# Token groups of 64, 64, 69 and 69 chunks, and the SSM's products of one round in alternating PSUM banks

## The chip, the core and the metric

The kernel runs on one core of a Trainium2 chip. The metric is the device time of one execution in microseconds (us), lower is better; "the time" of a kernel is the median of its runs. TensorE is called PE here (its weight loads PEld), VectorE DVE, ScalarE ACT, GpSimd POOL; SP is the engine whose queue issues all the DMAs.

## The reference

One step of a hybrid decoder layer over 2064 prompt tokens (16 meta tokens and 2048 others) and 8 running sequences of 8 tokens, 1024 features, all in float32.

```python
xn = rmsnorm(h, norm_gain)
u_s, z_s, u_p, z_p, gates = split(xn @ w_in)            # six blocks of 1024 columns
y_s = S5(u_s)        # 64 groups of 16 channels, 64 complex states each, then gelu and a GLU (w_glu)
y_p = pool(u_p)      # causal means over 2, 4, 8, 16 tokens, then pool_mix and pool_scale
merged = g_s * ((y_s * silu(z_s)) @ w_branch_ssm) + g_p * ((y_p * silu(z_p)) @ w_branch_pool)
out = rmsnorm(h + merged @ w_out, final_norm_gain)      # and the new SSM states and pool rows
```

## The kernel before

**Tokens.** Eight consecutive tokens make a chunk. The 258 chunks of the prompt and the 8 running sequences (one chunk each) are 266 columns, cut into four groups `g0` to `g3` of 69, 69, 64 and 64 chunks (`GROUPS`), so of 552, 552, 512 and 512 token columns. The first two chunks of `g0` are the meta tokens; only the SSM's input `us` and the pool's input `up` are computed for them, so the other products of `g0` have 67 chunks, 536 columns. A group of more than 512 columns does each matmul in two halves (`nh = 2`: 2 x 276, or 2 x 268 in `g0`), one of at most 512 in one piece (`nh = 1`). The last group holds the running sequences, and does its last three output units in two halves (`HD`), so that the end of one half can overlap the other.

**Units.** The work of a group is a row of units: 80 products with a 128 x 1024 block of weights (`us`, `up`, `zp`, `gate`, `brp`, `zs`, `glu`, `brs`, `out`, eight of each, and eight more gates), and four smaller `mix` units. A product is done in three parts to keep float32's precision (`mm3`: high weights by high and by low data, low weights by high data). So a unit is 8 x 3 matmuls, or 8 x 3 pairs of halves; a `mix` unit is 12. That makes 80 x 24 + 4 x 12 = 1968 such steps for each group. ACT makes each weight block's high part (`wh`, L106), DVE its low part (`wl`, L207), two units ahead. PE's results lie in three accumulators (`acc`); what reads one is called its post (`po`, `H`, `E`, ...), and a unit can't start before the post of the third unit back is done.

**Order.** Everything is written out in one order by hand: the `us` units of `g1` and of `g0`, then the rest of `g0`, of `g1`, `g2`, `g3`. The `us` units of `g2` and `g3` lie within `g0`. Other work is put between the matmuls of a unit (`between`):
- The matrices stage (`batches`, lines 349 to 458): beside `g0`'s pool units (`up`, `zp`, `mix`), 16 batches build the SSM's per-group matrices. For each, DVE, POOL and PE do a fixed set of operations (`bt`, `ct`, `t`, `t4b`, `ps_bt`, `ps_k`) that does not depend on the groups' sizes.
- The SSM (lines 463 to 625): 32 pairs of channel groups, in two rounds (`ROUNDS`). Round 0 covers the chunks of `g0` and `g1` (138 columns) and runs within `g0`, round 1 covers `g2` and `g3` (128) and runs within the last units of `g0`, in `g1` and in the first part of `g2`. A pair goes through steps of a pipeline, one tick each: load; the product x (`st_x`, PSUM tile `sx`); turn (`st_turn_a`, `st_turn_v`: ACT and DVE read `sx`); scan; swap; rot; state (POOL writes `sS`); the product y (`st_y`, tile `sy`); out (`st_out`: ACT reads `sy`, SP stores it). In each tick the steps in `EARLY` come first (the readers `st_out` and `st_turn_*`), those in `LATE` after them (`st_y`, then `st_x`). `sx` and `sy` have one PSUM bank each, so the x of a pair waits until DVE has read the x of the pair before, and y until ACT has.

SP's queue issues its DMAs in the order of the program, and each waits for its buffer. In round 1 the running sequences' old states `s0` were loaded with the pair's input, behind it in the tile `su`, and POOL copied them into `sS`.

Of the kernel before, what the change touches and what calls it, by code (L numbers as in the profile page):

```python
# [34 lines left out]
RK = (2.0 * DM) ** (2.0 / 3.0)  # L35


GROUPS = [(0, 69), (69, 69), (138, 64), (202, 64)]
GOFF = [T * k0 for k0, _ in GROUPS]

ROUNDS = [(0, 138), (138, 128)]


W_US, W_ZS, W_UP, W_ZP, W_GS, W_GP, W_GLU, W_BRS, W_BRP, W_OUT = range(0, 80, 8)
# [45 lines left out]
def hybrid_step(ctx, tc, a):  # L90
# [393 lines left out]
        return rows.rearrange("(q c) t k -> (c t) q k", q=2)  # L484

    def st_load(g, q):
        x = stile("su", 5, g.kn + (NS if g.last else 0))
        u = x[:, :, :g.kn]
        for i in (2 * g.i, 2 * g.i + 1):
            k = GROUPS[i][0] - ROUNDS[g.i][0]  # L490
            SY.dma_start(u[:, :, k:k + GROUPS[i][1]], chans(us_d[i], q))
        if g.last:
            SY.dma_start(x[:, :, g.kn:], a["s0"][:, 0, two(q)])
        mb = stile("smb", 2, P)
        SY.dma_start(mb, mat_d[q, :, 0])
        pr[q].update(u=u, mb=mb, s0=x[:, :, g.kn:])

    def st_phase(g, q):
        ph, n = stile("sph", 4), stile("scc", 4)
# [17 lines left out]
    def st_x(g, q):  # L517

        d = pr[q]
        d["px"] = sw["sx"][:, :, :g.kn]  # L520
        for j in range(2):
            PE.matmul(d["px"][:, j], d["mb"][:, j], d["u"][:, j], start=True, stop=True)  # L522

# [51 lines left out]
    def st_state(g, q):  # L575

        d = pr[q]
        c, w, kp = d["c"], d["s"], g.kp
        s = stile("sS", 3, g.kn)
        now = state[:, two(q)].unsqueeze(2)  # L580
        if g.last:
            G.tensor_copy(s[:, :, kp:], d["s0"])
        G.tensor_copy(s[:, :, 0:1], now)
        G.tensor_tensor(s[:, :, 1:kp], c[:, :, 1:kp], w[:, :, 1:kp], ALU.subtract)
        G.tensor_tensor(now, c[:, :, kp:kp + 1], w[:, :, kp:kp + 1], ALU.subtract)
        d["S"] = s

    def st_y(g, q):
        d = pr[q]
        d["py"] = sw["sy"][:, :, :g.kn]  # L590
        for j in range(2):
            m = slice(j * P, (j + 1) * P)
            PE.matmul(d["py"][:, j], d["m"][:, 0, m], d["u"][:, j], start=True, stop=False)  # L593
            PE.matmul(d["py"][:, j], d["m"][:, 1, m], d["S"][:, j], start=False, stop=True)  # L594
# [40 lines left out]
    class Group:  # L635
# [42 lines left out]
        def proj(self, w, xh, xl, halves=None, meta=False):  # L678


            ps = self.acc()
            n = self.HD if halves else self.ND
            nk = len(xh)
            for k in range(nk):
                between(k / nk)
                outs, xs = [], []
                for h in halves or range(self.nh):
                    m = n + (T * self.km if meta and h else 0)
                    outs.append(ps[:, h, :m])
                    xs.append([v[k][:, h * n:h * n + m] for v in (xh, xl)])  # L690
                mm3(outs, [x[:, k * P:(k + 1) * P] for x in w], xs, k == 0, k == nk - 1)
            return ps
# [63 lines left out]
        def rms_sum(self, ss, halves=None, early=False):  # L756

            n = self.HD if halves else ss.shape[1] // self.nh
            if early:
                ps = [psb.tile([P, 512], F32, tag=t, name=t)[:, :n] for t in ("bx", "by")]  # L760
            else:
                acc = self.acc()
                ps = [acc[:, h, :n] for h in range(self.nh)]
            for h in halves or range(self.nh):
                PE.matmul(ps[h], onesm, ss[:, h * n:(h + 1) * n], start=True, stop=True)  # L765
            self.ps = ps
# [54 lines left out]
        def up_post(self, fb, ps):  # L821
            wi = fb // 2
            kn, kp, last = self.kn, self.kp, self.last
            ke = 2 + kp + (3 * NS if last else 0)
            own = sw["r"] if last else tmp
            E = self.t(own, "E", 2, shape=[P, T, ke])
            if last:
                es = E[:, :, 2 + kp:].rearrange("p t (s k) -> p t s k", k=3)
                G.tensor_copy(es[:, :, :, 0:2], self.hs.pop(fb))
            if last:  # L830
                src = ps[:, 0, :self.N].rearrange("p (t k) -> p t k", k=kn)
                A.activation(E[:, :, 2:2 + kp], src[:, :, :kp], AF.Copy)
                A.activation(es[:, :, :, 2:3], src[:, :, kp:].unsqueeze(3), AF.Copy)
            else:
                for dst, src in self.parts(E[:, :, 2:2 + kp], ps):
                    A.activation(dst, src, AF.Copy)  # L836
            G.tensor_copy(E[:, :, 0:2], hist[:, fb])
            if last:
                new = self.t(own, "np", 2, shape=[P, T, 2 + NS])
                G.tensor_copy(new[:, :, 0:2], E[:, :, kp:kp + 2])  # L840
                G.tensor_copy(new[:, :, 2:].unsqueeze(3), es[:, :, :, 2:3])
                SY.dma_start(a["np"][:, fb], new)
            else:
                G.tensor_copy(hist[:, fb], E[:, :, kp:kp + 2])  # L844
            cur = E
            for step in range(wi + 1):
                d = 1 << step
                nxt = self.t(own, f"w{step % 2}", 1, shape=[P, T, ke])

                if d < 4:  # L850
                    n, o, c = (x.rearrange("p t k -> p (t k)") for x in (nxt, cur, cur))
                    i = d * ke + step
                    V.tensor_tensor(n[:, i:], o[:, i:], c[:, step:T * ke - d * ke], ALU.add)  # L853
                elif d < T:
                    V.tensor_tensor(nxt[:, d:, 1:], cur[:, d:, 1:], cur[:, :T - d, 1:], ALU.add)
                else:
                    V.tensor_tensor(nxt[:, :, 2:], cur[:, :, 2:], cur[:, :, 1:ke - 1], ALU.add)
                if d < T:
                    V.tensor_tensor(nxt[:, :d, 1:], cur[:, :d, 1:], cur[:, T - d:, :ke - 1], ALU.add)
                cur = nxt  # L860
            iw = 1.0 / WINDOWS[wi]
            po = self.t(tmp, "po", 2)
            p3 = po.rearrange("p (t k) -> p t k", k=self.kd)
            km = self.km
            V.scalar_tensor_tensor(p3[:, :, :kp - km], cur[:, :, 2 + km:2 + kp], iw, E[:, :, 2 + km:2 + kp],
                                   ALU.mult, ALU.subtract)
            if last:
                cs = cur[:, :, 2 + kp:].rearrange("p t (s k) -> p t s k", k=3)
                V.scalar_tensor_tensor(p3[:, :, kp:], cs[:, :, :, 2], iw, es[:, :, :, 2],
                                       ALU.mult, ALU.subtract)  # L870
            self.po[fb] = po
# [352 lines left out]
    def to_ssm():  # L1224
# [2 lines left out]
        sw["g"] = ctx.enter_context(tc.tile_pool(name="gp", bufs=1))  # L1227
        sw["p"], sw["end"] = pool("sw")
        ps = ctx.enter_context(tc.tile_pool(name="ps", bufs=1, space=PSUM))
        for n in ("sx", "sy"):  # L1230
            sw[n] = ps.tile([P, 2, 160], F32, name=n)

    def end_ssm():
        final_states()
# [225 lines left out]
```

## Time and profile before

| | |
|---|---|
| three runs | 2082.71, 2083.03, 2084.15 us; median 2083.03 us |
| profiled execution | 2081.01 us, its span 2079.2 us |
| granted TensorE clock, mean | 0.996 |
| busy share of the span: PE, DVE, ACT, POOL | 98%, 63%, 48%, 26% |
| share of PE in the chain that ended last | 73% |

The span runs from the first to the last instruction; the execution's own time has 1.8 us more around it. The profile's matmul durations overlap, so PE's rate is read from the distance between starts, not from the busy time.

### The profile page before, as it was taken

The page shows a single profiled execution, that of the slowest core. Times are in us where ns is not written, and L with a number is a line of the kernel's source. Part 1 is how long each engine was busy: PE and PEld are TensorE (multiplying, and loading weights), DVE is VectorE, ACT ScalarE, POOL GpSimd, SP SyncE. Part 2 cuts the span into 40 slices and gives each one's busy share as a digit, 9 for nine tenths or more (in the row PEclk, how much of TensorE's full clock was granted, in tenths as well). Part 3 has the DMA queues.
Part 4 walks back from the last instruction along what each step waited for, and adds up shares of the span by engine and source line. Part 5 has one row for each costly group of instructions (what it writes and reads, how often), then busy time and mean ns, then how long its engine had stood idle before and what let it go on. Part 6 is the DMA issues. An engine that isn't in the chain of part 4 may idle for free.

```text
span 2079.2 us, 33846 instructions
## 1 busy us (share of the span) xinstructions
PE 2041.4 (98%) x13024; PEld 1852.7 (89%) x13024; DVE 1315.7 (63%) x1848; ACT 1002.8 (48%) x1597; POOL 547.7 (26%) x716
## 2 busy tenths in 40 slices
PE   8999999999999999999999999999999999999998
PEld 8999899978999999999999998888888888888887
DVE  7789958898645776555764686535534676354444
ACT  5335469877446553366575653333432433243322
POOL 1156516574411430022332340012200200021001
PEclk9999999999999999999999999999999999999999
DMA  5446657587534643245445544334333443343233
GB/s 204 140 127 182 177 168 213 159 244 199 154 96 146 172 134 119 97 124 137 120 121 153 166 137 140 97 119 144 107 117 117 138 148 102 101 130 103 92 106 97
DMA packets 230466, 288.16 MB, mean 139 GB/s; under 512 B 115872, under 2 KB 160544, under 8 KB 230304
## 3 DMA queue, kind: packets, MB, share of 16 engines
q1 hardware_dynamic: 230304, 285.99, 45.9%
q8 instruction: 103, 1.69, 0.3%
q14 instruction: 59, 0.48, 0.1%
HBM read 242.61 MB, written 40.95 MB: 136 GB/s over the span
## 4 chain that ended last, share of the span: by engine, by line
PE 73%; DVE 1%; ACT 0%; DMA 0%; issue 0%; DVEq 0%; POOL 0%; ACTq 0%; POOLq 0%
PE acc L131 24%; PE acc L133 24%; PE acc L129 24%; PE sy L593 1%; PE sy L594 1%; PE sx L522 1%; DVE al L115 0%; DMA ys<-sS 0%; PE acc L765 0%; ACT wh L106 0%; DVE xr L1070 0%; DVE G L999 0%; DVE sg L998 0%; DVE wl L207 0%; DVE G L1017 0%
## 5 line engine op out<-in xcount | busy, mean ns | idle before, releaser
L129 PE MATMUL acc<-ah,wh 128*128 128x276 f32 (+4 forms) x3864 | 1047.5, 325 | 7.8 <-DVE po L798 3.3
L131 PE MATMUL acc<-al,wh 128*128 128x276 f32 (+4 forms) x3864 | 1040.7, 323 | 1.4 <-DVE al L115 0.7
L133 PE MATMUL acc<-ah,wl 128*128 128x276 f32 (+4 forms) x3864 | 1037.2, 322 | 1.2 <-DVE wl L207 1.2
L106 ACT ACTIVATE wh<-raw 128x1024 fp32r<-128x1024 f32 (+1 forms) x336 | 347.1, 1034 | 797.0 <-PE acc L131 502.9
L129 PEld LDWEIGHTS acc<-ah,wh 128*128 128x128 f32 x3864 | 647.6, 189 | 70.5 <-issue 4.4
L131 PEld LDWEIGHTS acc<-al,wh 128*128 128x128 f32 x3864 | 648.6, 189 | 58.2 <-DVE al L115 1.4
L133 PEld LDWEIGHTS acc<-ah,wl 128*128 128x128 f32 x3864 | 646.1, 188 | 55.3 <-DVE wl L207 1.8
L207 DVE TENSOR_TENSOR wl<-raw,wh 128x1024 fp32r<-128x1024 f32 (+1 forms) x336 | 420.8, 1253 | 126.9 <-ACT wh L106 126.3
L545 POOL TENSOR_TENSOR sXw<-sXw,sph 128x276 f32<-128x276 f32 (+1 forms) x64 | 50.1, 783 | 337.3 <-ACT sXw L531 337.2
L889 DVE SCALAR_TENSOR_TENSOR H<-H,acc 128x512 f32<-128x512 f32 (+2 forms) x64 | 44.9, 702 | 79.5 <-ACT H L888 79.5
L987 DVE SCALAR_TENSOR_TENSOR H<-po,H 128x512 f32<-128x512 f32 (+2 forms) x32 | 23.5, 733 | 113.3 <-ACT po L985 113.3
L115 DVE TENSOR_TENSOR al<-H,ah 128x512 fp32r<-128x512 f32 (+2 forms) x104 | 78.8, 790 | 14.9 <-ACT ah L106 14.0
L541 DVE TENSOR_TENSOR sX<-sx,scc 128x276 f32<-128x276 f32 (+1 forms) x64 | 27.0, 421 | 94.4 <-ACT sX L534 69.2
L963 POOL TENSOR_SCALAR w<-w 128x512 f32<-128x512 f32 (+2 forms) x32 | 28.7, 898 | 214.0 <-ACT w L962 213.8
L106 ACT ACTIVATE ah<-H 128x512 fp32r<-128x512 f32 (+2 forms) x88 | 50.9, 602 | 55.9 <-DVE H L919 39.6
L553 DVE TENSOR_TENSOR_SCAN sX<-r,state,sX 128x138 f32<-128x138 f32 (+1 forms) x128 | 73.0, 611 | 2.3
L1028 POOL TENSOR_TENSOR ss<-ss,po 128x512 f32<-128x512 f32 (+2 forms) x25 | 41.5, 1661 | 116.7 <-ACT po L1024 102.8
L853 DVE TENSOR_TENSOR w<-E 128x497 f32<-128x497 f32 (+2 forms) x32 | 23.6, 739 | 70.5 <-ACT E L836 49.5
L940 DVE SCALAR_TENSOR_TENSOR G<-sg,acc 128x512 f32<-128x512 f32 (+2 forms) x32 | 22.4, 701 | 72.0 <-PE acc L133 69.8
L844 POOL COPY hist<-E 128x16 f32<-128x16 f32 x24 | 14.1, 585 | 201.2 <-ACT E L836 201.0
L104 POOL TENSOR_SCALAR ah<-G 128x512 fp32r<-128x512 f32 (+2 forms) x16 | 15.1, 948 | 182.4 <-DVE sg L998 146.4
L998 DVE SCALAR_TENSOR_TENSOR sg<-sg,acc 128x512 f32<-128x512 f32 (+2 forms) x32 | 22.4, 700 | 63.1 <-PE acc L133 63.1
(239 smaller groups left out, 2203.9 us busy)
## 6 DMA issues: line engine op xcount, KB each, us to landing
raw<-in_wb SPq DMA_DIRECT2D x318, 512.0 KB, 3.6
smc<-mat_d SPq DMA_DIRECT2D x64, 256.0 KB, 3.6
smb<-mat_d SPq DMA_DIRECT2D x64, 128.0 KB, 2.6
H<-in_xb SPq DMA_DIRECT2D x22, 256.0 KB, 4.0
xr<-in_xb SPq DMA_DIRECT2D x19, 256.0 KB, 3.8
H<-in_xb SPq DMA_DIRECT2D x16, 276.0 KB, 5.3
us<-po SPq DMA_DIRECT2D x16, 276.0 KB, 4.3
su<-us SPq DMA_DIRECT2D x64, 69.0 KB, 3.1
```

Of the source, the lines that this page charges most:

```text
L106: A.activation(out, in_, AF.Copy)
L115: V.tensor_tensor(l, x, h.bitcast(F32), ALU.subtract)
L129: PE.matmul(out, wh, xh, start=first, stop=False)
L131: PE.matmul(out, wh, xl, start=False, stop=False)
L133: PE.matmul(out, wl, xh, start=False, stop=last)
L207: V.tensor_tensor(l[:, c], r[:, c], h[:, c].bitcast(F32), ALU.subtract)
L541: V.tensor_tensor(d["x"], d["px"][:, :, :g.kp], d["c"][:, :, 1:g.kp + 1], ALU.mult)
L545: G.tensor_tensor(d["xw"], d["xw"], d["s"][:, :, 1:g.kp + 1], ALU.mult)
L553: V.tensor_tensor_scan(x[:, j], r8[:, i].to_broadcast([P, g.kp]), x[:, j], state[:, i], ALU.mult, ALU.add)
L889: V.scalar_tensor_tensor(self.v3(out), self.v3(out), 1.0, self.pv(ps), ALU.add, ALU.mult)
L963: G.tensor_scalar(q, q, 0.044715, 1.0, ALU.mult, ALU.add)
L1028: (G if h is None else V).tensor_tensor(self.ss[:, c], self.ss[:, c], s, ALU.add)
```

## The change

The group sizes are turned round, 64, 64, 69, 69. `g0` and `g1` now do each product in one piece (496 columns in `g0` without, 512 with the meta tokens; 512 in `g1`), `g2` and `g3` in two halves of 276. The SSM's rounds have 128 and 138 columns. In round 0 the x and the y of one pair have 4 x 128 columns of float32 together, one whole bank, and the pairs use two banks in turn; in round 1 the same two tiles are one for x and one for y, as before. The states `s0` come by a DMA straight into `sS`, at the state step, and POOL's copy goes. What the pool branch copies out of PSUM for the last group is done by halves, and the sums of squares of the first two groups use one early bank in place of two.

```diff
-GROUPS = [(0, 69), (69, 69), (138, 64), (202, 64)]
+GROUPS = [(0, 64), (64, 64), (128, 69), (197, 69)]
-ROUNDS = [(0, 138), (138, 128)]
+ROUNDS = [(0, 128), (128, 138)]
...
     def st_load(g, q):
-        x = stile("su", 5, g.kn + (NS if g.last else 0))
-        u = x[:, :, :g.kn]
+        u = stile("su", 5, g.kn)
...
-        if g.last:
-            SY.dma_start(x[:, :, g.kn:], a["s0"][:, 0, two(q)])
...
+    def bank(g, q, y):
+        if g.kn <= P:
+            return sw["b"][q % 2][:, 2 * y:2 * y + 2, :g.kn]
+        return sw["b"][y].rearrange("p (j a) k -> p j (a k)", j=2)[:, :, :g.kn]
...
-        d["px"] = sw["sx"][:, :, :g.kn]
+        d["px"] = bank(g, q, 0)
...
         if g.last:
-            G.tensor_copy(s[:, :, kp:], d["s0"])
+            SY.dma_start(s[:, :, kp:], a["s0"][:, 0, two(q)])
...
-        d["py"] = sw["sy"][:, :, :g.kn]
+        d["py"] = bank(g, q, 1)
...
-                    m = n + (T * self.km if meta and h else 0)
+                    m = n + (T * self.km if meta and h == self.nh - 1 else 0)
...
-                ps = [psb.tile([P, 512], F32, tag=t, name=t)[:, :n] for t in ("bx", "by")]
+                ps = [psb.tile([P, 512], F32, tag=t, name=t)[:, :n] for t in ("bx", "by")[:self.nh]]
...
-                src = ps[:, 0, :self.N].rearrange("p (t k) -> p t k", k=kn)
-                A.activation(E[:, :, 2:2 + kp], src[:, :, :kp], AF.Copy)
-                A.activation(es[:, :, :, 2:3], src[:, :, kp:].unsqueeze(3), AF.Copy)
+                tn = T // self.nh
+                for h in range(self.nh):
+                    ts, src = slice(h * tn, (h + 1) * tn), ps[:, h, :self.N].rearrange("p (t k) -> p t k", k=kn)
+                    A.activation(E[:, ts, 2:2 + kp], src[:, :, :kp], AF.Copy)
+                    A.activation(es[:, ts, :, 2:3], src[:, :, kp:].unsqueeze(3), AF.Copy)
...
-        for n in ("sx", "sy"):
-            sw[n] = ps.tile([P, 2, 160], F32, name=n)
+        sw["b"] = [ps.tile([P, 4, P], F32, name=f"sb{i}") for i in range(2)]
```

First place, PE in round 0 of the SSM, one tick between two units of `g0`, before. The names in brackets are what a row waits for: DMA landings (DMAHW), and the engines.

```order
1666 L133 MATMUL acc<-ah,wl 128x268 x2
1667 L593 MATMUL sy<-su,smc 128x138 [waits DMAHW0_49,Activation_49]
1668 L594 MATMUL sy<-sS,smc 128x138 [waits Pool_49]
1669 L593 MATMUL sy<-su,smc 128x138
1670 L594 MATMUL sy<-sS,smc 128x138
1671 L522 MATMUL sx<-su,smb 128x138 [waits DMAHW2_49,DMAHW3_49,DMAHW1_49,DVE_49]
1672 L522 MATMUL sx<-su,smb 128x138
1673 L129 MATMUL acc<-ah,wh 128x268 [waits PE_49]
1674 L129 MATMUL acc<-ah,wh 128x268
```

The same tick in the changed kernel:

```order
1211 L597 MATMUL sb_2591<-su,smc 128x128 [waits DMAHW0_49,DVE_49]
1212 L598 MATMUL sb_2591<-sS,smc 128x128 [waits Pool_49]
1213 L597 MATMUL sb_2591<-su,smc 128x128
1214 L598 MATMUL sb_2591<-sS,smc 128x128
1215 L526 MATMUL sb_2591<-su,smb 128x128 [waits DMAHW3_49,DMAHW2_49,DMAHW1_49]
1216 L526 MATMUL sb_2591<-su,smb 128x128
1217 L129 MATMUL acc<-ah,wh 128x496 [waits PE_49]
1218 L131 MATMUL acc<-al,wh 128x496
```

The products keep their place. x no longer waits for DVE, and y waits for DVE's reading of this bank, which belongs to the tick before, in place of ACT's reading in the same tick. Each matmul of the unit is one row of 496 columns where two of 268 stood.

Second place, DVE in the matrices stage, around one batch of `batches` beside an `up` unit of `g0`, before (`bt`, `ct` are the batch's, `wl` the weights', `w` and `po` the unit's post).

```order
226 L389 TENSOR_TENSOR bt<-bt,t_2066 128x512
227 L393 TENSOR_TENSOR ct<-craw,tT_107 128x512
228 L207 TENSOR_TENSOR wl<-raw,wh 128x1024
229 L853 TENSOR_TENSOR w_2118<-E 128x497
230 L859 TENSOR_TENSOR w_2118<-E 128x70
231 L853 TENSOR_TENSOR w_2121<-w_2118 128x425
232 L859 TENSOR_TENSOR w_2121<-w_2118 128x2x70
233 L865 SCALAR_TENSOR_TENSOR po<-w_2121,E 128x536
234 L399 TENSOR_TENSOR ct<-ct,t4b 128x512
```

The same rows in the changed kernel:

```order
220 L389 TENSOR_TENSOR bt<-bt,t_1491 128x512
221 L393 TENSOR_TENSOR ct<-craw,tT_107 128x512
222 L207 TENSOR_TENSOR wl<-raw,wh 128x1024
223 L859 TENSOR_TENSOR w_1530<-E 128x462
224 L865 TENSOR_TENSOR w_1530<-E 128x65
225 L859 TENSOR_TENSOR w_1533<-w_1530 128x395
226 L865 TENSOR_TENSOR w_1533<-w_1530 128x2x65
227 L871 SCALAR_TENSOR_TENSOR po<-w_1533,E 128x496
228 L399 TENSOR_TENSOR ct<-ct,t4b 128x512
```

No row moved. Five of these rows got some 7% narrower, the rows of the batch and of the weights did not.

Third place, SP's queue in one tick of round 1, before (`su`, `smb` are the pair's input and matrix, `smc` the matrices of y).

```order
466 L535 DMA xs_d<-sX 128x2x8
467 L566 DMA smc<-mat_d 128x512
468 L491 DMA su<-us_86 128x2x64
469 L491 DMA su<-us_87 128x2x64
470 L493 DMA su<-in_s 128x2x8
471 L495 DMA smb<-mat_d 128x256
```

And in the changed kernel:

```order
472 L539 DMA xs_d<-sX 128x2x8
473 L586 DMA sS<-in_s 128x2x8
474 L570 DMA smc<-mat_d 128x512
475 L490 DMA su<-us_86 128x2x69
476 L490 DMA su<-us_87 128x2x69
477 L492 DMA smb<-mat_d 128x256
```

The small load of `s0` moved up from the late to the early part of the tick, ahead of the load of `smc`, and into another tile.

## Rows read from the trace of the kernel before

**Rows 1.** The page: busy time and share of each engine.
```profile
PE 2041.4 (98%) x13024; PEld 1852.7 (89%) x13024; DVE 1315.7 (63%) x1848; ACT 1002.8 (48%) x1597; POOL 547.7 (26%) x716
```

**Rows 2.** Windows by stage: length, busy us of PE, PEld, DVE, ACT, POOL; clock; DMA.
```profile
0.00:78.00 78.00, 69.04 (x482) 66.03 (x483) 56.88 (x111) 36.45 (x59) 6.12 (x8) 0.98 0.48 163
...
146.00:260.00 114.00, 109.63 (x969) 103.23 (x966) 110.86 (x135) 55.97 (x91) 70.31 (x67) 0.99 0.64 178
...
290.00:420.00 130.00, 125.54 (x947) 120.02 (x946) 108.33 (x171) 114.37 (x205) 69.27 (x110) 1.00 0.61 176
420.00:545.00 125.00, 118.06 (x674) 101.85 (x673) 100.78 (x158) 86.41 (x164) 65.13 (x93) 1.00 0.76 219
545.00:2069.00 1524.00, 1520.70 (x9184) 1364.08 (x9182) 866.24 (x1158) 668.97 (x1009) 299.35 (x405) 1.00 0.41 123
2069.00:2079.20 10.20, 0.70 (x2) 0.30 (x2) 5.89 (x11) 0.89 (x2) 2.61 (x3) 0.62 0.45 154
```

**Rows 3.** Waits of PE, 0 to 78 us: total, times, longest.
```profile
PE acc L129 <- DVE po L798: 2.9, 2, 1.8
PE acc L129 <- DVE al L115: 2.0, 1, 2.0
PE acc L133 <- DVE wl L207: 1.2, 1, 1.2
```

**Rows 4.** Waits of PE, 146 to 262 us (the matrices stage).
```profile
PE ps_k L411 <- DVE ct L399: 2.6, 1, 2.6
PE acc L129 <- DVE H L889: 1.7, 1, 1.7
```

**Rows 5.** Waits of PE, 288 to 545 us (round 0 of the SSM).
```profile
PE sy L593 <- DMA smc<-mat_d: 4.7, 3, 2.4
PE sx L522 <- DVE sX L541: 2.5, 2, 1.6
PE sy L593 <- ACT sS L599: 1.7, 3, 0.9
PE sy L593 <- ACT wh L106: 1.0, 1, 1.0
```

**Rows 6.** Waits of PE, 545 us to the end, the longest row.
```profile
PE sx L522 <- DVE sX L541: 2.8, 1, 2.8
```

**Rows 7.** Timeline of PE: starts of pairs of 268, pairs of 276, single 512 (46, 46, 55 rows).
```profile
552.33 0.41 PE L129 MATMUL acc<-ah,wh 128*128 128x268 f32 x2
563.36 0.41 PE L129 MATMUL acc<-ah,wh 128*128 128x268 f32 x2
...
1004.18 0.42 PE L129 MATMUL acc<-ah,wh 128*128 128x276 f32 x2
1015.61 0.42 PE L129 MATMUL acc<-ah,wh 128*128 128x276 f32 x2
...
1560.05 0.40 PE L129 MATMUL acc<-ah,wh 128*128 128x512 f32 x1
1572.59 0.39 PE L129 MATMUL acc<-ah,wh 128*128 128x512 f32 x1
```

**Rows 8.** DVE, 146 to 260 us, by form: busy us, mean ns; four of 18 groups.
```profile
L207 DVE TENSOR_TENSOR wl<-raw,wh 128x1024 fp32r<-128x1024 f32 x13 | 22.3, 1717 | 0.0
L389 DVE TENSOR_TENSOR bt<-bt,t 128x512 f32<-128x512 f32 x14 | 19.7, 1409 | 1.5
...
L853 DVE TENSOR_TENSOR w<-w 128x425 f32<-128x425 f32 x6 | 6.4, 1066 | 0.2
...
L857 DVE TENSOR_TENSOR w<-w 128x552 f32<-128x552 f32 x1 | 0.7, 732 | 0.0
```

**Rows 9.** Windows of 10 us, columns as in rows 2.
```profile
30.00:40.00 10.00, 8.15 (x53) 7.96 (x52) 9.23 (x20) 3.27 (x5) 1.38 (x1) 0.83 0.48 140
60.00:70.00 10.00, 8.04 (x64) 7.85 (x63) 7.38 (x15) 4.00 (x10) 0.00 (x0) 1.00 0.26 82
240.00:250.00 10.00, 8.04 (x58) 7.46 (x59) 9.82 (x12) 2.59 (x4) 4.23 (x3) 0.83 0.60 153
```

**Rows 10.** Timeline, 294 to 301 us: one x waits for the turn of the pair before.
```profile
295.60 0.39 ACT L531 ACTIVATE sXw<-sx 64x276 f32<-64x276 f32 x1
296.02 0.45 DVE L541 TENSOR_TENSOR sX<-sx,scc 128x276 f32<-128x276 f32 x1 [5.24 <-ACT sXw L531]
296.52 0.74 PE L522 MATMUL sx<-su,smb 128*128 128x138 f32 x4 [1.58 <-DVE sX L541]
```

More of the change, by code (lines that the diff above doesn't have):

```diff
@@ L491, in st_load @@
             SY.dma_start(u[:, :, k:k + GROUPS[i][1]], chans(us_d[i], q))
-        if g.last:
-            SY.dma_start(x[:, :, g.kn:], a["s0"][:, 0, two(q)])
         mb = stile("smb", 2, P)
         SY.dma_start(mb, mat_d[q, :, 0])
-        pr[q].update(u=u, mb=mb, s0=x[:, :, g.kn:])
+        pr[q].update(u=u, mb=mb)
+    def bank(g, q, y):
+        if g.kn <= P:
+            return sw["b"][q % 2][:, 2 * y:2 * y + 2, :g.kn]
+        return sw["b"][y].rearrange("p (j a) k -> p j (a k)", j=2)[:, :, :g.kn]
     def st_phase(g, q):
```

## The prediction

> **What bounds the kernel now.** I read the page first, then the windows by stage, then the waits of PE in each stage, and the timelines last. PE is busy for 98% of the span [rows 1], so the time is the sum of PE's matmuls and of the places where PE stands still. The windows say where those are [rows 2]: from 545 to 2069 us PE is busy for 1520.7 of 1524 us, and what it waits there is one 2.8 us [rows 6]. All other losses lie in the first 545 us and in the last ten. There are three kinds. At the start PE waits for chains that end on DVE, 6.1 us in the three largest rows [rows 3]. In the matrices stage, 146 to 260 us, DVE is busy for 110.9 of 114 us, and PE waits for it for 4.3 us [rows 2, 4]: DVE sets the pace there, and PE is only just slower. In round 0 of the SSM, 290 to 545 us, PE waits 9.9 us in four rows [rows 5]; 2.5 us are x waiting for DVE's reading of the last x and 1.7 us y waiting for ACT's reading of the last y. One such wait is drawn out in the timeline: ACT reads `sx` until 295.99, DVE until 296.47, and x starts at 296.52 [rows 10]. The 4.7 us for the load of `smc` are another matter: it is a transfer issued too late in its tick.
>
> **The matmul sum.** The rate is the distance of starts [rows 7]: 11.03 us for 45 pairs of 268 columns, 0.2451 us each; 11.43 / 45 = 0.2540 for a pair of 276; 12.54 / 54 = 0.2322 for one of 512. No 496 runs before. Half a pair of 268 takes 0.1226, so from 268 to 512 a column costs (0.2322 - 0.1226) / 244 = 0.45 ns, and 496 columns take 0.2250. Now by group. `g0` has 1584 steps without the meta tokens, 0.2451 to 0.2250, -31.8 us; its 16 units with them are 384 steps of 552 columns (taken as a pair of 276), then 512: -8.4. What `g1` gains, 1968 x 0.0218 = 42.9 us, `g2` loses. `g3` loses 1896 x 0.0218 = 41.3, and 72 steps of its halved output units go from 2 x 256 (2 x 0.1172 by the same slope) to 2 x 276, +1.4. The sum is **+2.5 us**: the columns are the same 2112 in all, and only the small differences between shapes are left. Bounds: at the steeper slope between 268 and 276, 0.56 ns a column, 496 takes 0.2233 and the sum is -0.2; if 496 costs as much as 512, it is +13.9. I take the slope over the long distance, between whose ends 496 lies.
>
> The Trainium skill (TensorE: Matmul & The Clock Gate, Back-to-back issue gap) gives a warm matmul N / 2.4 ns plus about 2.5 ns. By it 512 columns would take 216 ns where the rows show 232, every column would cost the same, and the sum would be the 72 matmuls that are saved, -0.2 us (an estimate). The rows decide.
>
> The 12 products of a pair in the SSM have 138 and 128 columns in the one order and in the other, so their sum stays.
>
> **The matrices stage.** Beside the batches PE has 13 weight blocks of 1024 [rows 8] and two `mix` units, 13 x 24 + 2 x 12 = 336 steps, which shrink by 336 x 0.0201 = 6.8 us; the sum above counts that as gained. DVE hardly shrinks: of its 110.9 us the token-wide operations are 43 (12 of the 18 groups, the first and the last of them shown), and 7% of them is 3 us; the weights' 22.3 and the batch's `bt` 19.7 stay [rows 8]. So DVE needs 108 us, and 111 with the 3 us of gaps that it has now, while PE needs 114 - 4.3 - 6.8 = 103. The stage ends at 108 to 111, a gain of 3 to 6 in place of 6.8. I charge **+3.0 us**, nearer to the present density. Bounds: 0, if the three accumulators give enough slack; 6.8, if nothing of it comes back. PE would be seen waiting 6 to 8 us there instead of 4.3.
>
> **The start.** In 78 us PE has some 223 steps (482 matmuls less those of the warm-up and the sums of squares, two to a step), 4.9 us shorter. What ends its waits are chains on ACT and DVE, in which the token-wide operations shrink by 7% and the weights' don't; DVE is busy for 56.9 us [rows 2], and I take 60% of that as token-wide (a choice), 2.4 us. A part of the gap between 4.9 and 2.4 is hidden, as PE doesn't wait at every unit. Charge **+1.5 us**, bounds 0 and 4.9.
>
> **Round 0.** With two banks in turn x waits for nothing on DVE, and y for the tick before. The two rows of 2.5 and 1.7 go: **-4.2 us**. The third, y with ACT's `wh` named, is y's load or state and I leave it. What is late next is the load of `smc`: it is issued behind the store of `sS`, which waits for ACT, and that is not touched; 0.5 us more for a unit of `g2` or `g3` helps it little. Bounds: nothing, if these 4.2 us move into that wait; -9.9, if all four rows go.
>
> **Edits at nothing.** The load of `s0` stays one DMA per pair but stands in front of `smc` and waits for the `sS` of three pairs back, whose store was issued a tick before. Queued behind it on SP are `smc`, `su` and `smb`. The cover is round 1's slow pace, 32 pairs spread beyond 545 us, where PE waited for no load [rows 6]; without it the nearest price is the longest wait for `smc`, 2.4 us [rows 5], once or a few times. The copies from PSUM by ACT (fewer in `g0` and `g1`, more in `g2` and `g3`) lie under PE, ACT being busy for 669 of 1524 us. Round 1's x still waits for the turn before; the 2.8 us [rows 6] stay. `g1` now has units shorter by 0.5 us and pairs of 138 beside them, but DVE has 866 of 1524 us there. The **end** grows: after the last unit come 10.2 us [rows 2] with 5.9 us of DVE on 256 columns, now 276, **+0.4 us**.
>
> **Clock.** Two of the long waits at the start were followed by a stretch at the lower of the two levels, 1.2 GHz: the mean is 0.83 in 30 to 40 and in 240 to 250 us, but 1.00 in 60 to 70 with a wait as long [rows 9]. Ten us at 0.83 lose 1.7. More waits may bring one such stretch more, or the same number; I add nothing, and give it 1.7 us in the range.
>
> **Sum.** +2.5 + 3.0 + 1.5 - 4.2 + 0.4 = +3.2 us. Against the profiled execution (2081.0 us, span 2079.2 and 1.8 around it) that is 2084.2; the median of the runs lies 2.0 above it, at 2083.0, so I forecast **2086.2 us**.
>
> **Rivals.**
> 1. *The banks pay more than I count, and it gets faster.* PE then is not held at x, ACT and DVE fall less behind, and the loads of `smc` are issued earlier, so that all 9.9 us of rows 5 go; the matrices stage and the start charge nothing. 2083.0 + 2.5 + 0.4 - 9.9 = 2076.0. For it: all four waits end in the same few units. Against it: the 4.7 us are the distance from the issue to the use, not a bank, and DVE's 97% in the matrices stage. It decides if fewer than 2 us of rows 5 stay. The Trainium skill (Perfetto Trace Analysis, Matmuls) has the rule on its side: independent groups of matmuls should rotate through banks, and larger matmuls are more efficient. Chance 0.14.
> 2. *DVE doesn't charge.* The accumulators and the posts two units late swallow the shorter units: no +3.0 and no +1.5, 2081.7, no change. For it: PE waits only twice in the stage now [rows 4]. Chance 0.22.
> 3. *The first half of round 0 gets bound.* From 290 to 420 us ACT is busy for 114.4 and DVE for 108.3 of 130 us [rows 2], beside 18 units of `g0` that lose 432 x 0.0201 = 8.7 us. If their chains don't shrink with them, as in the matrices stage, most of that stays: + 7 us, 2093. Against it: with 5% off, ACT would have 109 of 121, 90%, less than the 97% at which DVE shows as the bound. Chance 0.22.
> 4. *As forecast*, own range 2083 to 2090: 0.42.
>
> **Chances.** 0.2% is about what a measurement of this kernel can tell, 4.2 us: faster is below 2078.8, slower above 2087.2. Slower: all but a little of 3, and nearly half of 4, 0.42. Faster: 1 and the edge of 2, 0.15. The same: 0.43. The range from 2077.5 to 2094 leaves out half of 1 and a third of 3, some 0.15 in all; the unknown of 496 columns, the bounds of the charges and one stretch of slow clock lie within it, except the far end of +13.9.
>
> **What would show it.** Waits of PE in round 0: no `sx` on `sX`, none of `sy` on `sS`, `smc` still there with 4 to 5 us (right); or none at all (rival 1). Matrices stage: PE idle for 6 to 8 us with DVE at 97% or more (right), or unchanged (rival 2). The distance of starts of 496 columns: 0.225 us. From 290 to 420 of before: new waits on DVE or ACT would be rival 3. The forecast is wrong in size above all if 496 columns run at another rate, since 1584 steps hang on it: 1 ns is 1.6 us.

## The result and the profile after

The changed kernel takes 2104.06 us (median of four runs, 2099.85 to 2105.59), beside 2083.59 for the kernel before on the same chip: 1.0097 of it, 95% interval 1.0084 to 1.0110. It is slower by 20 us, and outside the range. The profiled execution took 2099.85 us, its span is 2098.0; it was the fastest of the four, with a mean granted clock of 0.995 where the three others had 0.991 to 0.994.

The page has the same share for PE as [rows 1]:

```profile
PE 2049.6 (98%) x12950; PEld 1861.1 (89%) x12950; DVE 1314.2 (63%) x1845; ACT 1003.1 (48%) x1596; POOL 529.1 (25%) x684
```

Windows by stage of the changed kernel, columns as in [rows 2]:

```profile
0.00:72.00 72.00, 62.14 (x251) 47.03 (x252) 52.75 (x103) 34.98 (x57) 5.72 (x8) 1.00 0.50 168
136.00:250.00 114.00, 106.49 (x650) 83.94 (x648) 111.86 (x138) 55.20 (x86) 73.74 (x70) 0.97 0.63 176
278.00:405.00 127.00, 118.86 (x684) 103.89 (x683) 104.47 (x171) 113.39 (x206) 64.08 (x109) 1.00 0.58 178
405.00:540.00 135.00, 130.21 (x936) 125.05 (x936) 108.83 (x170) 91.45 (x172) 65.53 (x98) 0.99 0.74 214
540.00:2087.00 1547.00, 1540.66 (x10046) 1428.32 (x10044) 865.72 (x1147) 669.52 (x1016) 282.36 (x370) 1.00 0.40 121
2087.00:2098.00 11.00, 0.98 (x4) 0.30 (x2) 6.56 (x12) 0.92 (x2) 2.79 (x3) 0.75 0.46 155
```

The second row is the one to read. It is a window of the same length at nearly the same place of the program as in [rows 2], the matrices stage, 10 us earlier on the clock of the run. PE's busy time in it fell by 3 us; DVE's 110.9 us became 111.9. PE's waits from 130 to 252 us (total, times, longest) are now 7.0 us in three rows, where [rows 4] had 4.3:

```profile
PE acc L129 <- DVE H L895: 3.0, 1, 3.0
PE ps_k L411 <- DVE ct L399: 2.7, 1, 2.7
PE acc L129 <- DVE H L925: 1.3, 1, 1.3
```

PE's waits over the whole of the changed kernel (total, times, longest):

```profile
PE sb L597 <- DMA smc<-mat_d: 9.1, 5, 3.2
PE acc L133 <- DVE wl L207: 4.6, 6, 1.5
PE acc L129 <- DVE po L802: 4.6, 3, 2.1
PE sb L526 <- DVE sX L545: 4.5, 5, 3.0
PE acc L129 <- DVE H L895: 3.0, 1, 3.0
PE acc L129 <- DVE al L115: 3.0, 1, 3.0
PE ps_k L411 <- DVE ct L399: 2.7, 1, 2.7
```

In round 0 x now waits for no `sX` and y for no `sS` of ACT. The load of `smc` has grown from 4.7 us [rows 5] to 9.1, all of it in round 0. All 4.5 us of x waiting for `sX` lie in round 1, where one wait of 2.8 stood [rows 6]. There PE waits for no load, so the moved load of `s0` costs nothing that the trace shows.

**Where the time went.** I number the units from 0 to 338 and divide the span at the first matmuls of units 16, 39, 73, 108, 189 and 338, which the timelines show. The column "products" is what PE's matmuls alone should change: their number by the distance of starts of each shape. It is good to about half a us, since 0.5 ns in a distance is 0.4 us in the longest rows.

| stage (units) | before | after | change | products | not got back |
|---|---|---|---|---|---|
| `us` of g1 and g0 (0 to 15) | 118.9 | 112.3 | -6.6 | -8.2 | 1.6 |
| matrices (16 to 38) | 159.1 | 154.4 | -4.7 | -10.3 | 5.6 |
| round 0 (39 to 72) | 258.2 | 257.2 | -1.0 | -2.7 | 1.7 |
| rest of g0, round 1 begins (73 to 107) | 220.6 | 208.4 | -12.2 | -16.1 | 3.9 |
| g1 and five units of g2, round 1 (108 to 188) | 509.3 | 477.3 | -32.0 | -34.8 | 2.8 |
| rest of g2, g3 (189 to 337) | 799.5 | 874.0 | +74.5 | +74.4 | 0.1 |
| the last unit and the end | 13.7 | 14.4 | +0.7 | +0.2 | 0.5 |
| span | 2079.2 | 2098.0 | +18.8 | +2.5 | 16.3 |

The wide groups g2 and g3 cost what their products cost, in a part of the kernel where PE waits for almost nothing. The narrow g0 and g1 don't give that back: nearly all that is lost is a saving that didn't come.

A part of the last column is PE's clock. In the trace the granted clock falls to the lower of its two levels, 1.2 GHz, for short stretches. Before, there are two ahead of the end, from 33.6 and 241.8 us. After the change there are four, from 184.5, 232.3, 413.2 and 604.4 us. By the distances of the matmuls in them each costs 1.5 to 1.6 us. So the slow clock gives the start 1.5 us back, takes 1.5 us each in the matrices, in round 0 and in units 73 to 107, and is 3.1 of the 16.3 us.

The rate of 496 columns, which no row before showed, from PE's timeline of the changed kernel:

```profile
553.10 0.39 PE L129 MATMUL acc<-ah,wh 128*128 128x496 f32 x1
...
563.31 0.39 PE L129 MATMUL acc<-ah,wh 128*128 128x496 f32 x1
```

That is 10.21 us for 45 distances, 0.2269; over the 1475 of the trace that are below 0.26 us the mean is 0.2250, as estimated.

### The profile page after: what moved, and what is told of

It is laid out like the page before. It is cut to its first block, busy times and chain, and to the rows that moved or that the text cites. A ratio compares the mean times of both kernels' runs of the same rounds, so it can differ in the third digit from the quotient of the medians.

```text
span 2098.0 us, 33649 instructions
## 1 busy us (share of the span) xinstructions
PE 2049.6 (98%) x12950; PEld 1861.1 (89%) x12950; DVE 1314.2 (63%) x1845; ACT 1003.1 (48%) x1596; POOL 529.1 (25%) x684
## 4 chain that ended last, share of the span: by engine, by line
PE 75%; DVE 6%; ACT 4%; issue 2%; DMA 2%; SPq 0%; POOL 0%; DVEq 0%; POOLq 0%; ACTq 0%
PE acc L129 24%; PE acc L131 24%; PE acc L133 24%; DVE wl L207 1%; DVE al L115 1%; PE sb L597 1%; PE sb L598 1%; PE sb L526 1%; DMA mat_d<-mp 1%; DVE sX L557 1%; DVE sph L577 0%; DVE sph L513 0%; DVE sX L545 0%; ACT wh L106 0%; DVE sX L554 0%
## 5 line engine op out<-in xcount | busy, mean ns | idle before, releaser
L129 PE MATMUL acc<-ah,wh 128*128 128x276 f32 (+2 forms) x3840 | 1053.3, 327 | 13.2 <-DVE po L802 4.6
L133 PE MATMUL acc<-ah,wl 128*128 128x276 f32 (+2 forms) x3840 | 1038.7, 324 | 4.6 <-DVE wl L207 4.6
L131 PE MATMUL acc<-al,wh 128*128 128x276 f32 (+2 forms) x3840 | 1040.4, 324 | 1.6 <-DVE al L115 0.8
L549 POOL TENSOR_TENSOR sXw<-sXw,sph 128x256 f32<-128x256 f32 (+1 forms) x64 | 47.9, 748 | 335.7 <-ACT sXw L535 335.6
L895 DVE SCALAR_TENSOR_TENSOR H<-H,acc 128x552 f32<-128x552 f32 (+2 forms) x64 | 44.9, 702 | 81.0 <-ACT H L894 81.0
L115 DVE TENSOR_TENSOR al<-H,ah 128x552 fp32r<-128x552 f32 (+2 forms) x104 | 78.5, 788 | 13.4 <-ACT ah L106 12.4
L969 POOL TENSOR_SCALAR w<-w 128x552 f32<-128x552 f32 (+2 forms) x32 | 28.6, 893 | 228.0 <-ACT w L968 227.8
L106 ACT ACTIVATE ah<-H 128x552 fp32r<-128x552 f32 (+2 forms) x88 | 50.9, 602 | 55.5 <-DVE H L925 39.4
L557 DVE TENSOR_TENSOR_SCAN sX<-r,state,sX 128x128 f32<-128x128 f32 (+1 forms) x128 | 75.0, 625 | 2.3
L1034 POOL TENSOR_TENSOR ss<-ss,po 128x552 f32<-128x552 f32 (+2 forms) x25 | 41.3, 1652 | 122.1 <-ACT po L1030 118.3
```

The source lines that it names most:

```text
L106: A.activation(out, in_, AF.Copy)
L115: V.tensor_tensor(l, x, h.bitcast(F32), ALU.subtract)
L129: PE.matmul(out, wh, xh, start=first, stop=False)
L131: PE.matmul(out, wh, xl, start=False, stop=False)
L133: PE.matmul(out, wl, xh, start=False, stop=last)
L549: G.tensor_tensor(d["xw"], d["xw"], d["s"][:, :, 1:g.kp + 1], ALU.mult)
```

## The experiments

Theory 1: the order of the groups costs the time. g0 and g1 stand beside work that doesn't shrink with them (the matrices on DVE, the weights, the SSM's ticks and loads), and a shorter unit there only waits. Theory 2: the banks cost it. PE, no longer held at x, comes early to y and to `smc`. All experiments are changes to the changed kernel; "old order" is its code with groups of 69, 69, 64, 64. Times are medians, ratios are to the kernel before (2083.0 to 2083.6 us on each chip), with 95% intervals.

### Order or banks

One bank for x and one for y in both rounds, with the changed groups:

```diff
     def bank(g, q, y):
-        if g.kn <= P:
-            return sw["b"][q % 2][:, 2 * y:2 * y + 2, :g.kn]
         return sw["b"][y].rearrange("p (j a) k -> p j (a k)", j=2)[:, :, :g.kn]
```

> The changed groups, but one bank for x and one for y in both rounds. Theory 1 (the loss comes from the order of the groups: units of g0 and g1 get 7% shorter beside work that doesn't): as slow as the changed kernel, 2101 to 2107 us; waits of x for DVE come back in round 0, the waits for the load of smc fall below 9.1 us. Theory 2 (the banks in turn cost: PE, no longer held at x, stands at y instead): the 17 us of added waits go and the matmul sum of +2.5 and the tail stay, 2086 to 2089 us.

The groups of before with all other edits:

```diff
-GROUPS = [(0, 64), (64, 64), (128, 69), (197, 69)]
+GROUPS = [(0, 69), (69, 69), (138, 64), (202, 64)]
-ROUNDS = [(0, 128), (128, 138)]
+ROUNDS = [(0, 138), (138, 128)]
```

> Everything of the change but the sizes: groups of 69, 69, 64, 64, so round 1 now has the 128 columns and the two banks in turn, and round 0 one bank for each kind. Theory 1: nothing to lose, 2081 to 2086 us; the 2.8 us of x waiting for DVE in round 1 go. Theory 2: the banks in turn cost in round 1 what they cost in round 0, 2090 us or more.

Only g1 narrow, and only g0 narrow (`(0, 69), (69, 64), (133, 69), (202, 64)` and `(0, 64), (64, 69), (133, 64), (197, 69)`, rounds of 133 and 133):

> Groups of 69, 64, 69, 64, two rounds of 133 columns with one bank for each kind: only g1 is narrow early. The matmul sum is that of before. Theory 1: the matrices stage and round 0 lie in g0 and lose nothing; of the changed kernel's losses the 0.2 us of g1's us units and the 2.8 us from unit 108 to 189 stay: 2084 to 2089 us. Theory 2: no banks in turn, no loss, 2082 to 2085 us.

> Groups of 64, 69, 64, 69, two rounds of 133 columns with one bank for each kind: only g0 is narrow early. The matmul sum is +2.5 us, the tail +0.6. Theory 1: start 2, matrices stage 5.7, round 0 2 and the rest of g0 4.3 us stay: 2083.6 + 17 = 2100, between 2096 and 2103 us. Theory 2: only the matmul sum and the tail, 2085 to 2089 us.

| | time | ratio | units 16 to 38 | 39 to 72 | 73 to 107 | 108 to 188 |
|---|---|---|---|---|---|---|
| changed kernel | 2104.06 | 1.0097 (1.0084 to 1.0110) | 154.4 | 257.2 | 208.4 | 477.3 |
| order alone | 2103.16 | 1.0093 (1.0077 to 1.0108) | 154.7 | 259.3 | 208.6 | 477.3 |
| old order, banks in round 1 | 2079.55 | 0.9979 (0.9971 to 0.9988) | 159.1 | 261.6 | 217.3 | 509.6 |
| only g1 narrow | 2088.23 | 1.0021 (1.0012 to 1.0030) | 159.0 | 261.0 | 222.3 | 476.3 |
| only g0 narrow | 2104.72 | 1.0099 (1.0086 to 1.0113) | 154.0 | 260.2 | 208.8 | 510.5 |

Theory 2 is out: without the banks in turn the loss is the same, and with them in the old order the kernel is faster than before, and than the 2081 us that theory 1 allowed. Theory 1 holds, and nearly all of the loss belongs to a narrow g0, a little more than I expected (2104.7 for at most 2103). A narrow g1 alone costs 4.7 us. The stages agree: where g0 is narrow the matrices take 154 us, where it is wide 159, and not the 10.3 us of its products in between.

PE's waits in round 0 of the kernel with the order alone show that the banks did what the change says:

```profile
PE sb L595 <- ACT sS L601: 4.9, 3, 2.5
PE sb L524 <- DVE sX L543: 3.7, 2, 2.5
...
PE sb L595 <- DMA smc<-mat_d: 1.1, 2, 0.8
```

With one bank for each kind PE waits 8.6 us for ACT and DVE and 1.1 for `smc`; with two in turn it waits 9.1 for `smc` (above) and nothing for the others. In round 1 of the old order the banks pay: from 540 to 2066 us the view of PE's waits lists no more than

```profile
PE acc L131 <- DVE al L115: 0.2, 1, 0.2
PE acc L769 <- DVE ss L1034: 0.2, 1, 0.2
```

The 2.8 us of [rows 6] are gone, and units 73 to 107 take 217.3 us for 220.6. Round 0, which has one bank for each kind in this order, takes 261.6 us in its profile for 258.2 before: it holds two slow stretches, from 297.8 and 468.5 us, and the profile before holds none there. So the profiled execution, 2081.08 us, shows no gain beside the 2081.01 before; the gain is that of the medians.

### The matrices stage

The addition of the two products of `bt` left out, in the changed and in the old order:

```diff
-            V.tensor_tensor(d["bt"], d["bt"], d["t4"], ALU.add)
```

> The changed kernel without DVE's addition of the two products in bt, 16 times 1.4 us in the matrices stage: the SSM's input matrices then hold one product alone. Theory D (DVE sets the pace in the matrices stage; PE's shorter units of g0 are lost there): with 22 us less DVE work the excess of PE over its matmuls in units 16 to 39 falls from 17.1 us to under 11, and the time to 2094 to 2099 us; the distance to the same cut in the old order is 18 to 20 us instead of 24.5. Theory E (the stage loses to something else, such as PE's clock or the loads): 2102 us or more, and the distance stays 24 us.

> Groups of 69, 69, 64, 64 with all other edits of the change, and the same addition in bt left out. Theory D: DVE is at its limit in this order too, but by less: 2074 to 2079 us. Theory E: 2079 to 2080 us, as with the addition.

2093.00 us (1.0038, 1.0025 to 1.0050) and 2071.22 us (0.9942, 0.9930 to 0.9954), both lower than theory D's ranges. Units 16 to 38 fall from 154.4 to 144.2 us and from 159.1 to 153.7. Between the two orders there are now 9.5 us in this stage, nearly the 10.3 of the products, where 4.7 were. So this stage's loss follows DVE. The slow stretches go with the waits: the stage had two in the changed order and one in the old, and has none in either now, which is 3 and 1.5 us of the fall. The distance of the two times is 21.8 us and not the 18 to 20 expected. In the profiles the old order's round 0 got shorter (261.6 to 256.8) and the changed order's longer (257.2 to 260.8), but of this 1.5 and 2.7 us are the clock: in the old order one slow stretch is left of two, and in the changed order slow clock from 402.5 and 446.9 us costs 4.3 us where one stretch cost 1.6. How much of what comes free ahead of round 0 is lost in it is therefore not shown.

Leaving the addition out takes work from DVE and a link from the batch's chain. Two edits tell these apart: the addition on POOL, and one more product on DVE that nothing waits for.

```diff
-            V.tensor_tensor(d["bt"], d["bt"], d["t4"], ALU.add)
+            G.tensor_tensor(d["bt"], d["bt"], d["t4"], ALU.add)
```

> The changed kernel with the addition in bt done by POOL in place of DVE: the work and the chain of the batch stay, DVE is relieved of 22 us in the matrices stage, POOL (busy for 74 of 114 us there) gets them. Theory D1 (DVE's load sets the pace of the stage): units 16 to 39 shrink from 154.4 us to 150 or less, 2095 to 2100 us. Theory D2 (what counted was that a link of the batch's chain went): POOL is as slow a link, 2102 to 2106 us.

> Groups of 69, 69, 64, 64 with all other edits of the change, and the addition in bt on POOL. Theory D1: 2072 to 2076 us, as far below 2079.5 as most of what leaving the addition out gave. Theory D2: 2078 to 2081 us.

```diff
             V.tensor_tensor(d["ct"], d["ct"], d["t4b"], ALU.subtract)
+            x = bg.tile([P, 4, GCH, 8], F32, tag="spare", name="spare")
+            V.tensor_tensor(x, d["c1"].unsqueeze(3).to_broadcast([P, 4, GCH, 8]),
+                            bc(tT1, b, slice(1, 9)), ALU.mult)
```

> The changed kernel with one more product on DVE in each batch of the matrices stage (the same as ct's, 0.73 us, into a tile that nothing reads): 11.7 us more DVE work, and no link more in the batch's chain. Theory D1 (DVE's load sets the pace): units 16 to 39 grow from 154.4 us by 9 to 12, to about 2115 us. Theory D2 (the batch's chain of links sets it): 0 to 3 us more, 2104 to 2107 us.

> Groups of 69, 69, 64, 64 with all other edits of the change, and the same product more on DVE. Theory D1: DVE has only about 3 us to spare in this order, so 7 to 11 us more than 2079.5, 2087 to 2090 us. Theory D2: 2079 to 2082 us.

On POOL it gets slower: 2107.02 us (1.0115, 1.0101 to 1.0129) and 2082.15 us (0.9991, 0.9983 to 1.0000), the stage 158.6 and 162.4 us. That fits neither theory, because DVE was hardly relieved (the last section). One more product on DVE settles it: 2115.66 us (1.0157, 1.0143 to 1.0171) and 2088.10 us (1.0031, 1.0019 to 1.0042); the stage grows by 11.5 us to 165.9 and by 11.0 to 170.1, for 16 times 0.68 = 10.9 us of added work that no one waits for. In the changed order the slow clock in the stage costs the same with and without it, 3 us. In the old order it costs 4.4 us for 1.5, which is 2.9 of the 11.0 us; the 8 that are left, and the 8.6 us in the medians, fit the 3 us that DVE was said to have to spare. DVE's load sets the pace. The windows of the stage, first without the addition, then with the added product, both in the changed order:

```profile
136.00:245.00 109.00, 107.61 (x671) 86.36 (x670) 105.25 (x127) 59.41 (x92) 70.62 (x70) 1.00 0.69 193
```

```profile
136.00:260.00 124.00, 106.91 (x632) 82.99 (x631) 121.83 (x149) 56.95 (x88) 76.31 (x68) 0.97 0.55 160
```

PE has 107 us of work in both. With DVE at 105 of 109 the two engines are level; with DVE at 122 of 124, PE waits.

### Round 0

The chain that holds PE at `smc`, from the timeline of the changed kernel (SP's rows are its DMA issues; L603 is ACT's copy of y, L597 the first matmuls of y):

```profile
305.86 0.38 SPq L604 DMA_DIRECT2D ys<-sS  x1
...
306.32 0.42 SPq L570 DMA_DIRECT2D smc<-mat_d  x1
...
310.54 0.46 PE L597 MATMUL sb<-su,smc 128*128 128x128 f32 x2 [0.95 <-DMA smc<-mat_d]
...
311.43 0.38 ACT L603 ACTIVATE sS<-sb 128x256 f32<-128x256 f32 x1
...
311.87 0.37 SPq L604 DMA_DIRECT2D ys<-sS  x1
...
312.33 0.42 SPq L570 DMA_DIRECT2D smc<-mat_d  x1
...
316.13 0.46 PE L597 MATMUL sb<-su,smc 128*128 128x128 f32 x2 [1.32 <-DMA smc<-mat_d]
```

The load goes out behind the store, the store waits for ACT's copy, and the load lands 3.8 to 4.2 us after its issue. Here a y follows the last by 5.6 us, in a unit that holds two ticks. Four edits cut at this chain, each in both orders. The load first in its tick:

```diff
-    EARLY = ((6, st_out), (2, st_turn_a), (2, st_turn_v), (3, st_swap), (2, st_turn_g),
-             (4, st_state), (0, st_phase), (1, st_wrap), (4, st_mat))
+    EARLY = ((4, st_mat), (6, st_out), (2, st_turn_a), (2, st_turn_v), (3, st_swap), (2, st_turn_g),
+             (4, st_state), (0, st_phase), (1, st_wrap))
```

> The changed kernel, but the load of smc is issued first in its tick, ahead of the store of the finished pair, so that it no longer waits for ACT's copy. Theory A (in ticks that follow each other in one unit the chain y, ACT's copy, store, load of smc, next y holds PE): the waits for smc fall from 9.1 us to under 5, and the time from 2104.1 to 2098 to 2101 us. Theory B (PE only arrives early, and something else of the pair is late next): the waits for smc fall, waits of y for POOL or ACT or of x for smb come in their place, and the time stays within 2102 to 2106 us.

> Groups of 69, 69, 64, 64 with the two banks in turn in round 1 (2079.55 us so far), and the load of smc first in its tick. Theory A: of the 3.9 us of waits for smc most go, 2075 to 2078 us. Theory B: as without, 2078 to 2081 us.

No load of `smc` but the first of each round:

```diff
-        d["m"] = stile("smc", 2, 2 * P)
-        SY.dma_start(d["m"], mat_d[q, :, 1:3].rearrange("p j q m -> p j (q m)"))
+        if q == 0:
+            sw["m"] = stile("smc", 1, 2 * P)
+            SY.dma_start(sw["m"], mat_d[q, :, 1:3].rearrange("p j q m -> p j (q m)"))
+        d["m"] = sw["m"]
```

> The changed kernel with the matrices smc loaded once in each round, for the first pair, and used for all: the SSM's outputs of the other pairs use wrong matrices, and 62 loads are gone. Theory A (the loads of smc are what holds PE in round 0): the 9.1 us of waits go and the excess of PE in units 39 to 73 falls from 18.3 to 11 us or less; 2094 to 2098 us. Theory B (the stage's length is set by the pair's chain through ACT, DVE and POOL, and the load only ends last): PE waits for ACT, POOL or smb instead, 2100 to 2105 us.

> Groups of 69, 69, 64, 64 with all other edits of the change, and smc loaded once in each round as in the run before it. Theory A: the 3.9 us of waits go, 2074 to 2077 us. Theory B: 2078 to 2081 us.

Two of ACT's five copies in a tick left out:

```diff
-        z, zw = d["x"], stile("sXw", 2, g.kp)
-        A.activation(zw[0:64], z[64:128], AF.Copy)
-        A.activation(zw[64:128], z[0:64], AF.Copy)
-        d["xw"] = zw
+        d["xw"] = d["x"]
```

> The changed kernel without the step swap, two copies of ACT for each pair, in which the halves of the state are exchanged; the rotation then uses the unexchanged halves. ACT was busy for 113 of 127 us in the first half of round 0. Theory C (ACT sets the pace of round 0): the excess in units 39 to 73 falls from 18.3 us by 5 or more, 2095 to 2099 us. Theory A or B of the loads and the pair's chain: 2101 to 2105 us.

> Groups of 69, 69, 64, 64 with all other edits of the change, without the step swap, as in the run before it. Theory C: a smaller gain than in the changed order, 2075 to 2078 us. Otherwise 2078 to 2081 us.

Fewer units with two ticks:

```diff
-BA, BB = 0.25, 0.0
+BA, BB = 0.75, 0.0
-    spread(rounds[0], lo, i, busy, BA)
+    spread(rounds[0], lo, i + 2, busy, BA)
```

> The changed kernel with round 0 spread over two units more and more evenly (a larger share for the units that also prepare g2 and g3), so that two units hold two ticks instead of six. Theory F (in such units the tick's loads can't keep up with PE): the 9.1 us of waits for smc fall under 4, and the time to 2097 to 2101 us. Theory G (the stage's length is set elsewhere): 2102 to 2106 us.

> Groups of 69, 69, 64, 64 with all other edits of the change, and round 0 spread in the same way. Theory F: 2074 to 2077 us. Theory G: 2078 to 2081 us.

| | changed order: time, ratio, units 39 to 72 | old order: time, ratio, units 39 to 72 |
|---|---|---|
| nothing cut | 2104.06, 1.0097 (1.0084 to 1.0110), 257.2 | 2079.55, 0.9979 (0.9971 to 0.9988), 261.6 |
| `smc` first | 2102.15, 1.0088 (1.0074 to 1.0102), 258.2 | 2079.25, 0.9975 (0.9966 to 0.9985), 259.9 |
| no `smc` | 2100.37, 1.0082 (1.0069 to 1.0094), 256.8 | 2078.91, 0.9980 (0.9972 to 0.9989), 260.1 |
| no swap | 2102.84, 1.0092 (1.0078 to 1.0106), 260.7 | 2079.47, 0.9977 (0.9968 to 0.9986), 257.8 |
| fewer double ticks | 2098.63, 1.0075 (1.0061 to 1.0089), 255.5 | 2080.72, 0.9986 (0.9977 to 0.9995), 259.5 |

`smc` first lowers its waits from 9.1 to 6.8 us, fewer double ticks to 5.6; neither goes as low as the theories of the load wanted. Without `smc` the next load of the same queue takes its place, PE's largest wait from 266 to 525 us being

```profile
PE sb L526 <- DMA smb<-mat_d: 7.1, 6, 2.8
```

In the old order no cut moves the time past its interval. By the program three units hold two ticks after that edit, where seven did. In the changed order fewer double ticks give the most, 5 us in the medians, about a quarter of the loss, with an interval that still touches that of the uncut kernel; this time lies in theory F's range, its waits and the old order's time don't. The other cuts give less. ACT's two copies are not it, nor is this one load. In all ten kernels round 0 lies between 255.5 and 261.6 us, while its products alone are 239 us in the changed order and 242 in the old. These lengths are of one profile each and hold different amounts of slow clock. By the distances of the matmuls it costs, from the top of the table, 1.6, 1.7, 3.2, 4.8 and 3.2 us in the changed order and 3.1, 1.6, 3.1, 1.5 and 5.0 in the old. Without it fewer double ticks make the stage 3 to 4 us shorter in both orders, 0.9 of it since eight products now stand in unit 73. What sets its length stays open.

## Why the prediction was wrong, step by step

- **The matmul sum** was right: +2.5 us by the measured distances, and 496 columns run at 0.2250 us.
- **The start** came out at 1.6 us for 1.5, by luck. In the stretch that I priced, units 0 to 8, nothing was lost: longer waits took about the 1.5 us that the slow stretch from 33.6 us had cost before. The loss lies in units 13 and 14, where PE waits 1.4 us for DVE's `wl` and waited for nothing before. **The end** was right, 0.5 for 0.4.
- **The matrices stage** had the right mechanism and too small a size: 5.6 us for 3.0, nearly all of it in the units that I priced (21 to 35). I saw that DVE would set the pace, and let more than half of the 6.8 us come back there. DVE's load, which the runs show to set the pace, came out at 111.9 of 114 us again, and 1.5 of the 5.6 us are one more stretch of slow clock, which I had put at nothing.
- **Round 0 failed.** I counted the waits of x for `sX` and of y for `sS` as gone, -4.2 us, and they are gone. But PE met the load of `smc` earlier instead. I wrote that 0.5 us more for a unit of g2 or g3 "helps it little". In g2's longer units (58 and 62) the 4.7 us of before did fall to 3.2; the other 5.9 of the 9.1 us are four waits in units 45 and 50, units of g0 with two ticks each, which got shorter and where PE waited for no `smc` before. The bound "nothing, if these 4.2 us move into that wait" is what happened, and 1.7 us more were not got back, of which 1.5 are the slow stretch from 413.2 us, behind the longest of these waits. In the order alone the same stage takes 259.3, with as much slow clock, so the banks were worth 2 us in the profiles; the medians, 2104.1 and 2103.2, don't show it.
- **Round 1 failed most.** It stood under the edits at nothing, with DVE's 866 of 1524 us as the reason: 6.7 us were not got back from unit 73 to 188. An average over 1500 us says nothing of the places where one x waits for one turn; that wait rose from 2.8 to 4.5 us. Units 73 to 107 take 208.8 us with g0 alone narrow, as in the changed kernel; units 108 to 188 take 476.3 with g1 alone narrow, nearly as in the changed kernel, and 510.5, nearly as before, with g1 wide. So the loss goes with the narrow group, except for one part: with g0 wide and g1 narrow units 73 to 107 take 222.3 us, more than before, and this too is a slow stretch behind a wait of 2.9 us for `sX`. The trace places some 5 of the 6.7 us: 1.5 for the slow stretch from 604.4 us, 1.7 for x's waits, 0.5 for a y that waits for ACT, and 1.2 for units 100 and 176, where PE waits for the split of its data (`ah`, `al`). Which operation sets each of these waits was not tried.
- **The clock** was forecast at nothing. Before, two windows of 10 us had a mean granted clock of 0.83 [rows 9]; now four have, each behind a wait of 2.7 to 3.2 us:

```profile
180.00:190.00 10.00, 6.97 (x46) 5.35 (x43) 9.90 (x10) 3.45 (x5) 7.28 (x7) 0.83 0.79 231
230.00:240.00 10.00, 7.38 (x35) 5.53 (x36) 9.79 (x14) 2.03 (x4) 4.23 (x3) 0.83 0.59 150
410.00:420.00 10.00, 7.35 (x46) 7.19 (x47) 6.83 (x16) 8.35 (x19) 5.79 (x11) 0.83 0.98 299
600.00:610.00 10.00, 6.96 (x27) 5.47 (x26) 7.41 (x11) 5.58 (x7) 1.97 (x3) 0.83 0.40 110
```

One of them in PE's timeline: a wait of 3.04 us, then seven matmuls of 496 columns 0.41 us apart, at 1.2 GHz, where 0.225 us is the mean.

```profile
603.56 0.74 PE L526 MATMUL sb<-su,smb 128*128 128x138 f32 x4 [3.04 <-DVE sX L545]
...
604.75 0.61 PE L133 MATMUL acc<-ah,wl 128*128 128x496 f32 x1
605.16 0.61 PE L129 MATMUL acc<-ah,wh 128*128 128x496 f32 x1
...
607.23 0.61 PE L133 MATMUL acc<-ah,wl 128*128 128x496 f32 x1
```

Seven times 0.19 is 1.3 us, and with the matmuls at both ends the stretch costs 1.5, so two more are 3.1 of the 16.3 us. The median is 4.2 us above the profiled execution, beside 2.6 for the kernel before, at lower mean clocks; that this is more such stretches was not seen in a trace of this kernel.

Of the rivals, the third had the right sign and a part of the place: it put + 7 us into the first half of round 0, and in units 39 to 57 3.4 us were not got back, where I had counted on a gain. But most of PE's waits there, 5.9 us, are for `smc`, and leaving out a part of ACT's 113 of 127 us changed little; DVE's load was not tried in this stage. The first, the banks pay, holds only in the other order: 4 us where the group sizes are left alone (with the other small edits, which weren't tried apart). The rule of the Trainium skill that stood beside it (Perfetto Trace Analysis, Matmuls: rotate independent groups of matmuls through banks) agrees with that run, and in the changed order with PE's waits for PSUM's readers, though not with the time. That kernel, 2079.55 us, beats both; `smc` first adds nothing that can be measured to it, 2079.25.

## What to carry to other kernels

Work that is moved from one part of a kernel to another is paid in full where PE is the bound, and saved only where PE is the bound: before sizes are turned round, look at which stages have a second engine level with PE, since there the saving is lost. A wait that is removed is worth its time only if the next operand of the same instruction has landed; look up when that was issued. And a busy share over a long stretch doesn't clear an edit: look at the few ticks in it that have a wait. Before two stage lengths are compared, look at the granted clock in both: here one slow stretch more or less, 1.5 us, was as large as several of the differences.

## What the hardware showed that I had not expected

Moving DVE's addition to POOL made rows of both engines slower. In the changed kernel the subtraction in `ct` (L399, two inputs of 128 x 512) takes 0.68 us each time. With the addition on POOL it takes 1.6 us in the five of 16 that run beside POOL's product `t` (L383), 0.93 in two beside products of 16 partitions, and 0.68 to 0.72 in the others. Two instances from the timelines of DVE and POOL of that kernel, the first beside a POOL product of two inputs, the second beside one of a single input:

```profile
163.51 1.11 POOL L383 TENSOR_TENSOR t<-b,tT 128x512 f32<-128x512 f32 x1
163.59 1.58 DVE L399 TENSOR_TENSOR ct<-ct,t4b 128x512 f32<-128x512 f32 x1 [0.41 <-POOL t4b L392]
...
173.10 1.26 POOL L385 TENSOR_SCALAR craw<-craw,cst 128x64 f32<-128x64 f32 x1
...
173.58 0.68 DVE L399 TENSOR_TENSOR ct<-ct,t4b 128x512 f32<-128x512 f32 x1
```

The weights' `wl` went from 1.72 to 2.30 us in the mean, and POOL's `t4b` from 1.48 to 1.95:

```profile
L392 POOL TENSOR_TENSOR t4b<-craw,tT 128x512 f32<-128x512 f32 x15 | 29.2, 1945 | 0.0
L207 DVE TENSOR_TENSOR wl<-raw,wh 128x1024 fp32r<-128x1024 f32 x12 | 27.6, 2296 | 0.0
```

So a part of the 22 us that were to leave DVE came back on its other rows: it is busy for 105.5 of 114 us, and now also waits 7 us for POOL. The Trainium skill (GPSIMD Engine Reference, Specifications) says that GpSimd shares its SBUF interfaces with VectorE, with contention for DVE instructions that have two SBUF inputs; these rows agree beside POOL's products of two inputs, while beside the operation with one input `ct` is as fast as alone. The same is to be read from [rows 8] before: 15 of the 16 additions in `bt` run beside POOL's product `t4b` and take 1.40 to 1.42 us, and the one that doesn't takes 0.69.
